# Two transformer blocks on one core: the durations, ranks and one root of a mixer planned while the program is built

## The chip, the core and the metric

The kernel runs on one core of a Trainium2 chip. The core has five engines with queues of their own: TensorE (PE, matrix products; its weight loads are shown as PEld), VectorE (DVE), ScalarE (ACT), GpSimd (POOL) and SyncE (SP, which here only issues transfers). The metric is the device time of one execution in microseconds (us). The median of three runs of the kernel before is 1177.67 us (1176.16 to 1180.08).

## The reference

The input is a sequence of 256 tokens with 1024 channels. It goes through two blocks of two layers each; every layer is a mixer and an MLP, each with a residual.

```python
# first block: even mixer, MLP, odd mixer, MLP, final norm
h = h + even_mixer(rms_norm(h, mix_norm_g[0]), ...)      # DSA: 8 heads; NSA: 8 heads in 2 groups
h = h + diff_mixer(rms_norm(h, mix_norm_g[1]), ...)      # 8 heads of two score maps
h = h + square(relu(rms_norm(h, mlp_norm_g[l]) @ w_up[l])) @ w_down[l]    # 1024 -> 4096 -> 1024
# second block, modulated by a conditioning vector: pooling mixer, MLP, MoBA attention, MLP, final norm
```

- The even mixer has two halves. In DSA an indexer of four small heads scores all keys, the 64 best of each query are kept, and eight heads attend to them. NSA adds three gated branches: attention to keys that a small MLP (`cmp_w1`, a gelu, `cmp_w2`) compresses from windows of 32 tokens, attention to selected blocks, and attention to a sliding window. With 256 tokens all blocks are selected and the window holds the sequence, so the last two are plain causal attention with keys of their own.
- The odd mixer subtracts a second softmax map, times a learned number, from a first: `a = p[:, :, 0] - lam_val * p[:, :, 1]`. Its output is normed for each head by a root mean square over 128 channels before the output product (`rms_norm(o, subln_g) * (1 - lambda_init)`). This is the sub-norm that the change speaks of.
- The second block's attention has 16 causal heads with a relative bias; with 256 tokens and blocks of 256 there are no past blocks to gather.

## The kernel before

Precision. All large products are made of three: each float32 operand is split into a high and a low half (`whi` and `wlo` of a weight, `xh` and `xl` of the activations), and high x high, low x high and high x low are summed in PSUM (`mm3`, line 383). The weights, 2048 columns of 128 partitions at a time, arrive by transfers from SP into a ring of four `raw` tiles; ACT makes `whi`, DVE makes `wlo` by subtraction, into rings of three. In the mixers a split is done in pieces of 512 columns. Attention itself (scores `sc`, transposes `pT` of the softmax, products `o`) is in plain float32.

Stages. After the first projection the program goes: even mixer, MLP 0, odd mixer, MLP 1, pooling, MLP 2, second block's attention, MLP 3. The MLPs (`mlp`, line 842) are written out in a fixed order, with 16 upward products (`pc`) and 16 downward ones (`dn`), and weight splits spread between their matmuls.

The plan. The three attention mixers have no order written by hand. While the program is built, each piece of work is a Python generator that yields before every group of instructions what it waits for. `Plan.run` (line 274) asks all generators for the earliest time at which their next step could start, takes those within a short tie (`TIE`, 0.12 us) of the earliest, and emits the step of the lowest rank among them. The instruction order that results is fixed; on the chip each engine works through its own queue in that order and waits on semaphores. What sets the order therefore is:

- `Clock` (line 47) and `Watched.cost` (line 141): an estimated time for each engine, advanced by an estimated duration for each instruction, plus a lag until another engine sees a result (`SYNC`, 0.08 us; 0.2 us after a matmul). Nothing of it is on the chip.
- the ranks: pairs of heads have their number in the order of attention, counted from 0 (`g_attend`, line 1061), and the front of that line its number plus 1.5; the projections and output products (`g_main`, `g_d`, `g_chain`; `Gather.gen`) have 80 to 85, so that they fill PE when attention waits; the join of the compressed branch (`g_join`, line 1392) 7; the sub-norm (`g_subln`) 5; the indexer's top-k (`g_top`) 9; the weight splits (`g_high`, `g_low`) -20 while less than 768 columns are ahead of PE, else 90.
- `soonest` (line 347), which picks DVE, ACT or POOL for scaling a softmax and for emptying a transpose, by the estimate plus a handicap for DVE (`DEAR`: 0.3, 0.5 and 0 us in the three mixers).

Details that the prediction's steps touch:

- In the even mixer a column is a pair of NSA heads, one of each group. Its selected and window branches are pairs 2c and 2c + 1. The compressed branch is added straight in PSUM if its softmax `pct` is there by then, else the column is evacuated and listed in `late`, and `g_join` adds the branch afterwards (product `oc`). The column is then split into `opA` and `opB`. The first output product (`dn` from `opA`) needs columns 0 and 1. The transposes of a softmax, the joins and other small products share one PSUM slot (`tp`).
- The compressing MLP (`hps`, in `g_main`, line 1168) multiplies 32 weight slices of 256 columns; four in a row go to four groups of 32 output rows.
- In the odd mixer `g_subln` runs once for each two heads, four times in all. It sums squares on PE (`oss`), computes the inverse root of four columns with `rsqrt_of` (line 649), spreads it over the partitions by transposes (`rw`), scales `osb` on DVE, and splits it on ACT and DVE for the output product. `rsqrt_of` starts from an integer guess (two DVE instructions) and does three Newton rounds on the engine it is given.
- In the second block's attention `g_chain` runs v of the first half, q and k of the second half, v of the second half, one after the other. Each ends with evacuations on ACT (`dv<-pj`, and `dq`, `dk` from `pc`) before the next begins. Pairs 0 to 3 are of the first half of the heads, 4 to 7 of the second.

The root's rounds, as they stand for an engine other than VectorE:

```python
        for _ in range(3):
            tt(t, y, y, ALU.mult, eng)
            tt(t, t, v, ALU.mult, eng)
            if eng is V:
                stt(y, t, 1.5, y, ALU.add, ALU.mult)
            else:
                eng.tensor_scalar(t, t, 1.5, None, op0=ALU.add)
                tt(y, t, y, ALU.mult, eng)
```

Of the kernel before, what the change touches and what calls it, by code (L numbers as in the profile page):

```python
# [38 lines left out]
INF = 1e30  # L39

DEAR = dict(V=0.3), dict(V=0.5), dict()
TOP_RANK, CMP_RANK = 9, -3

SPLIT_AHEAD = 768


class Clock:
# [3 lines left out]
    SYNC, DMA_RATE, DMA_LAG = 0.08, 3.2e5, 2.2  # L51

    def __init__(self):
        self.T = dict(PE=0.0, V=0.0, S=0.0, G=0.0)
        self.dma = 0.0
        self.mem, self.last = {}, {}

# [61 lines left out]

    def load(self, out, n_bytes):  # L120
# [14 lines left out]
class Watched:  # L135
# [5 lines left out]
    def cost(self, fn, out, ins, k, aps):  # L141
        size = Clock.size
        n = size(out)
        if self.name == "V":
# [4 lines left out]
            if fn == "tensor_tensor_reduce":  # L149
                return 0.25 + 1.0e-3 * n  # L150
# [4 lines left out]
            if fn == "reciprocal":  # L155
                return 0.15 + 0.7e-3 * n
            return 0.15 + 1.03e-3 * n
        if self.name == "S":
            return 0.2 + 0.79e-3 * n + 0.1 * (len(aps) > 2) + 0.19 * ("accum_out" in k)
        if fn == "tensor_scalar":  # L160
            return 0.2 + 3.4e-3 * n
        return 0.2 + 2.2e-3 * n

    def __getattr__(self, fn):
        real, clock = getattr(self.eng, fn), self.clock

        def call(*a, **k):
# [10 lines left out]
            if fn == "matmul":  # L178
                out, w, x = aps[:3]
                n = Clock.size(x)  # L180
                if x.dtype == F32:
                    dur, lag = max(0.11, n / 600.0 + 0.004), 0.2
                else:
                    dur, lag = 0.0092 + 0.4324e-3 * n, 0.2
                clock.note("PE", dur, [out], [w, x], lag)
            elif fn == "transpose":
                clock.note("PE", 0.109, aps[:1], aps[1:], 0.2)
# [60 lines left out]
class Plan:  # L248
# [3 lines left out]
    TIE = 0.12  # L252

    def __init__(self, clock):
        self.clock, self.q, self.n = clock, [], 0
# [18 lines left out]
    def run(self, until):  # L274
        while not until():
# [3 lines left out]
            self.advance(min((e for t, e in es if t <= m + self.TIE), key=lambda e: (e[0]() if callable(e[0]) else e[0], e[1])))  # L279
# [3 lines left out]
def two_blocks_kernel(ctx: ExitStack, tc: tile.TileContext, A, out):  # L283
# [25 lines left out]
    class Planned:  # L309

        on, dear = False, {}

        def __init__(self, dear):
            Planned.dear = dear

        def __enter__(self):
# [4 lines left out]
            for f in (g_high, g_low):  # L321
                plan.add(f(), lambda: -20 if W.ahead() < SPLIT_AHEAD else 90)
# [24 lines left out]
    def soonest(costs, *aps):  # L347

        return min(costs, key=lambda e: clock.at(e, *aps) + costs[e] + Planned.dear.get(e, 0.0))
# [679 lines left out]
    class Pair:  # L1029
# [5 lines left out]
        def scores(self):  # L1035

            t = clock.T["PE"]
# [15 lines left out]
    def attend(pairs):  # L1053
        at = [0]

        def front():
            return at[0] + 1.5
# [16 lines left out]
    def pv_pair(ps, pTs, vs, first, last):  # L1074

        t = clock.T["PE"]
# [4 lines left out]
        clock.T["PE"] = max(t, clock.T["PE"] - 0.55)  # L1081
# [86 lines left out]
    def g_main():  # L1168

        hps = None  # L1170
        for key in ORDER0[1:]:
            c = key[1]
            if key[0] == "w1":
# [4 lines left out]
                for it in range(2):  # L1178
# [923 lines left out]
```

## Time and profile before

| what | value |
|---|---|
| median of three runs | 1177.67 us |
| the profiled execution's own time | 1175.99 us |
| its span, first to last instruction | 1174.2 us |
| mean granted PE clock | 0.987 |
| PE busy | 1133.7 us, 97% |
| DVE, ACT, POOL busy | 855.7, 642.6, 41.4 us |
| moved by transfers | 243.91 MB, 208 GB/s in the mean |

An instruction row names engine, operation, output tile <- input tiles (buffer numbers left out), and shapes. Almost all instructions are issued by helpers, so their line is the same (L168); one goes by tiles. A busy PE is not a PE at full speed: matmuls overlap in the pipeline, so the distance from start to start is what one costs, and the granted clock (1.0 is full speed) says how fast the array ran. A float32 matmul of attention shows as several rows. In brackets behind a row stands the engine's idle time before it and the instruction that ended it.

### The profile page before, as it was taken

What the parts mean: (1) busy time and instruction counts of PE and PEld (TensorE: products, weight loads), DVE (VectorE), ACT (ScalarE), POOL (GpSimd) and SP (SyncE); (2) the same over time, 40 slices, a digit from 0 to 9 for tenths busy, and PEclk for the clock granted to TensorE, in tenths of its full rate; (3) what the DMA queues carried; (4) which work ended last, traced back from release to release, by engine and by line L of the source; (5) the groups of instructions that cost most, each with busy time, mean ns of one, the idle gap of its engine ahead of it and who ended that gap; (6) DMA issues with size and microseconds to landing.
All of it is one profiled execution on the core that took longest, in us unless ns stands there. A gap on an engine that the chain in (4) does not pass through costs nothing.

```text
span 1174.2 us, 21778 instructions
## 1 busy us (share of the span) xinstructions
PE 1133.7 (97%) x8760; PEld 1066.8 (91%) x8760; DVE 855.7 (73%) x1769; ACT 642.6 (55%) x1169; POOL 41.4 (4%) x113
## 2 busy tenths in 40 slices
PE   8997999999999998999999999999998999999997
PEld 6764899999987788999999999999996889999997
DVE  6967788777778776877787887777698558645554
ACT  6566664544455664545444664545466556555543
POOL 1200000000010203000000100000000000000000
PEclk9998999999999998999999999999999999999998
DMA  9520468888855434688888258888642444555530
GB/s 347 208 109 1 144 216 298 302 285 300 308 186 214 144 108 163 210 312 291 303 297 291 74 206 295 304 299 296 216 144 97 155 148 145 195 195 180 180 108 36
DMA packets 43476, 243.91 MB, mean 208 GB/s; under 512 B 5536, under 2 KB 6192, under 8 KB 21104
## 3 DMA queue, kind: packets, MB, share of 16 engines
q1 hardware_dynamic: 42336, 239.58, 58.3%
q0 software_dynamic: 896, 2.91, 0.8%
q8 instruction: 68, 1.11, 0.4%
q14 instruction: 32, 0.26, 0.1%
q10 hardware_dynamic: 144, 0.05, 0.0%
HBM read 241.44 MB, written 1.07 MB: 207 GB/s over the span
## 4 chain that ended last, share of the span: by engine, by line
PE 86%; DVE 7%; POOL 2%; ACT 2%; issue 1%; DMA 1%; SPq 0%; DVEq 0%; ACTq 0%; POOLq 0%
PE dn L168 37%; PE pc L168 32%; PE pj L168 9%; PE sc L168 2%; DVE wlo L168 2%; PE o L168 2%; PE pT L168 2%; POOL rs_t L168 1%; DMA raw<-in_in_c_dram 1%; DVE rs_t L168 1%; PE tps L168 1%; ACT whi L168 1%; DVE sq L168 0%; DVE x L168 0%; SPq L168 0%
## 5 line engine op out<-in xcount | busy, mean ns | idle before, releaser
L168 DVE TENSOR_TENSOR wlo<-raw,whi 128x1024 fp32r<-128x1024 f32 (+2 forms) x440 | 421.8, 997 | 123.6 <-ACT whi L168 123.1
L168 ACT ACTIVATE whi<-raw 128x1024 fp32r<-128x1024 f32 (+2 forms) x440 | 360.0, 869 | 128.2 <-PE dn L168 100.3
L168 PE MATMUL pc<-xh,whi 128*128 128x256 f32 (+1 forms) x1152 | 327.1, 284 | 1.4 <-DVE bias L168 1.4
L168 PE MATMUL pc<-xl,whi 128*128 128x256 f32 (+1 forms) x1152 | 325.8, 283 | 0.0
L168 PE MATMUL pc<-xh,wlo 128*128 128x256 f32 (+1 forms) x1152 | 325.1, 282 | 0.0
L168 PE MATMUL dn<-hh,whi 128*128 128x256 f32 x1024 | 289.7, 283 | 1.7 <-DVE bias L168 1.7
L168 PE MATMUL dn<-hl,whi 128*128 128x256 f32 x1024 | 289.4, 283 | 1.7 <-DVE hl L168 1.7
L168 PE MATMUL dn<-hh,wlo 128*128 128x256 f32 x1024 | 289.5, 283 | 0.0
L168 PEld LDWEIGHTS pc<-xh,whi 128*128 128x128 f32 x1152 | 217.7, 189 | 2.5 <-issue 2.3
L168 PEld LDWEIGHTS pc<-xh,wlo 128*128 128x128 f32 x1152 | 217.8, 189 | 0.0
L168 PEld LDWEIGHTS pc<-xl,whi 128*128 128x128 f32 x1152 | 217.8, 189 | 0.0
L168 PEld LDWEIGHTS dn<-hl,whi 128*128 128x128 f32 x1024 | 195.9, 191 | 2.1 <-DVE hl L168 2.1
L168 PEld LDWEIGHTS dn<-hh,whi 128*128 128x128 f32 x1024 | 195.9, 191 | 2.0 <-issue 2.0
L168 PEld LDWEIGHTS dn<-hh,wlo 128*128 128x128 f32 x1024 | 195.9, 191 | 0.0
L168 DVE SCALAR_TENSOR_TENSOR graw<-graw,cact 128x1024 f32<-128x1024 f32 x96 | 116.1, 1219 | 20.8 <-DMA graw<-in_w_mod_dram 20.7
L168 ACT ACTIVATE hh<-r 128x512 fp32r<-128x512 f32 x64 | 40.5, 633 | 127.1 <-DVE r L168 126.1
L168 PE MATMUL pj<-whi,xh 128*128 128x512 f32 (+2 forms) x208 | 86.1, 414 | 5.0 <-ACT whi L168 5.0
L168 ACT ACTIVATE r<-sc,bias 128x256 f32<-128x256 f32 x64 | 29.1, 502 | 112.5 <-DVE bias L168 112.5
L168 PE MATMUL pj<-wlo,xh 128*128 128x512 f32 (+2 forms) x208 | 80.8, 388 | 0.2 <-DVE wlo L168 0.2
L168 PE MATMUL pj<-whi,xl 128*128 128x512 f32 (+2 forms) x208 | 80.6, 387 | 0.0
L168 DVE TENSOR_TENSOR sc<-pc,rb 128x256 f32<-128x256 f32 x72 | 29.4, 417 | 36.6 <-PE pc L168 36.5
L168 PEld LDWEIGHTS pj<-whi,xh 128*128 128x128 f32 x208 | 39.6, 191 | 14.8 <-ACT whi L168 6.0
(262 smaller groups left out, 1290.6 us busy)
## 6 DMA issues: line engine op xcount, KB each, us to landing
raw<-in_up_dram SPq DMA_DIRECT2D x64, 1024.0 KB, 5.6
raw<-in_down_dram SPq DMA_DIRECT2D x64, 1024.0 KB, 5.4
graw<-in_w_mod_dram SPq DMA_DIRECT2D x96, 512.0 KB, 5.3
raw<-in_in_d_dram SPq DMA_DIRECT2D x12, 1024.0 KB, 5.5
raw<-in_w_out_dram SPq DMA_DIRECT2D x8, 1024.0 KB, 5.0
raw<-in_qk_dram SPq DMA_DIRECT2D x8, 1024.0 KB, 5.0
raw<-in_in_c_dram SPq DMA_DIRECT2D x7, 1024.0 KB, 8.9
raw<-in_v_dram SPq DMA_DIRECT2D x4, 1024.0 KB, 4.8
```

The source lines that it names most:

```text
L168: r = real(*a, **k)
```

## The change

- Durations: `Watched.cost` gets other constants for several instructions (among them the reciprocal, which now grows by 6.3 ns for each column, and fixed parts of POOL's); a float32 matmul counts at least 0.2 us; the lag after a matmul is 0.16, `SYNC` 0.05 us. A new function `turn` adds 0.09 us when PE goes from a split product to a float32 one or back. Where matmuls run side by side, the corrections are set anew.
- The parameters of the three mixers (`STRETCH`): handicap of DVE, columns ahead below which splits come first, distance of the front of the attention line, and the tie. Before they were 0.3, 0.5, 0 / 768 / 1.5 / 0.12 throughout.
- Ranks: top-k 9 to 12; `g_join` 7 to 3; the heads of the odd mixer's q and k from 20 to 8 (30 to 18 for the second half); `g_subln` 5 to 0; the projections of the second block's attention 85 to 3.
- The root in `g_subln` runs on VectorE.
- The compressing MLP's four row groups are emitted in one step, and three of four count 0.01 us each.

```diff
-DEAR = dict(V=0.3), dict(V=0.5), dict()
-TOP_RANK, CMP_RANK = 9, -3
-SPLIT_AHEAD = 768
+TOP_RANK, CMP_RANK = 12, -3
+STRETCH = (0.6, 384, 1.5, 0.3), (0.0, 1280, 1.5, 0.2), (0.3, 512, 2.5, 0.06)
...
-    SYNC, DMA_RATE, DMA_LAG = 0.08, 3.2e5, 2.2
+    SYNC, DMA_RATE, DMA_LAG = 0.05, 3.2e5, 2.2
...
+    def turn(self, kind):
+        if kind != self.kind:
+            self.T["PE"] += 0.09
+        self.kind = kind
...
             if fn == "reciprocal":
-                return 0.15 + 0.7e-3 * n
-            return 0.15 + 1.03e-3 * n
+                return 0.14 + 6.3e-3 * n
+            return 0.15 + 1.03e-3 * n if n < 64 or n > 256 else 0.24 + 0.92e-3 * n
...
         if fn == "tensor_scalar":
-            return 0.2 + 3.4e-3 * n
-        return 0.2 + 2.2e-3 * n
+            return 0.25 + 3.4e-3 * n
+        return 0.2 if n == 2 else 0.35 + 2.0e-3 * n
...
                 if x.dtype == F32:
-                    dur, lag = max(0.11, n / 600.0 + 0.004), 0.2
+                    dur = max(0.2, n / 600.0 + 0.004)
...
+                clock.turn(x.dtype == F32)
+                clock.note("PE", dur, [out], [w, x], 0.16)
...
         def scores(self):
...
-            clock.T["PE"] = t = max(t, clock.T["PE"] - 0.55)
...
-            clock.T["PE"] = max(t, clock.T["PE"] - 0.25)
+            clock.T["PE"] -= 0.5
...
         def front():
-            return at[0] + 1.5
+            return at[0] + Planned.front
...
-                        yield on("PE", w1(kk), L["X"][c])
+                        if k % 4 == 0:
+                            yield on("PE", *[w1(q) for q in range(kk, kk + 4)], L["X"][c])
+                        t = clock.T["PE"]
                         mm(hps[j:j + 32, c * 256:(c + 1) * 256], L["X"][c][:, 32 * k:32 * k + 32],
                            w1(kk), c == 0 and k < 4, k >= 12)
+                        if k % 4:
+                            clock.T["PE"] = t + 0.01
...
-            plan.add(g_join(c), 7)
+            plan.add(g_join(c), 3)
...
-        plan.add(g_flag(g_heads(ps, L["tabs"], 2 - 2 * j, halves_of(dst), (acc_p, tp_p)), ("qk"[j], half)), 20 + 10 * half)
+        plan.add(g_flag(g_heads(ps, L["tabs"], 2 - 2 * j, halves_of(dst), (acc_p, tp_p)), ("qk"[j], half)), 8 + 10 * half)
...
-            r = rsqrt_of(v, 4, G)
+            r = rsqrt_of(v, 4)
...
-                    plan.add(g_subln(hp), 5)
+                    plan.add(g_subln(hp), 0)
...
-        plan.add(g_chain(g_v(0), g_qk(1), g_v(1)), 85)
+        plan.add(g_chain(g_v(0), g_qk(1), g_v(1)), 3)
```

More of the change, by code (lines that the diff above doesn't have):

```diff
@@ L56, in __init__ @@
         self.mem, self.last = {}, {}
+        self.kind = False
     @staticmethod
@@ L149, in cost @@
             if fn == "tensor_tensor_reduce":
-                return 0.25 + 1.0e-3 * n
+                return 0.23 + 1.05e-3 * n
             if fn in ("max", "tensor_reduce"):
@@ L155, in cost @@
             if fn == "reciprocal":
-                return 0.15 + 0.7e-3 * n
-            return 0.15 + 1.03e-3 * n
+                return 0.14 + 6.3e-3 * n
+            return 0.15 + 1.03e-3 * n if n < 64 or n > 256 else 0.24 + 0.92e-3 * n
         if self.name == "S":
-            return 0.2 + 0.79e-3 * n + 0.1 * (len(aps) > 2) + 0.19 * ("accum_out" in k)
+            return 0.2 + 0.79e-3 * n + (0.1 if len(aps) > 2 and "accum_out" not in k else 0.13 * ("accum_out" in k))
+        if fn == "memset":
+            return 0.1 + 0.83e-3 * n
         if fn == "tensor_scalar":
-            return 0.2 + 3.4e-3 * n
-        return 0.2 + 2.2e-3 * n
+            return 0.25 + 3.4e-3 * n
+        return 0.2 if n == 2 else 0.35 + 2.0e-3 * n
     def __getattr__(self, fn):
@@ L181, in call @@
                 if x.dtype == F32:
-                    dur, lag = max(0.11, n / 600.0 + 0.004), 0.2
+                    dur = max(0.2, n / 600.0 + 0.004)
                 else:
-                    dur, lag = 0.0092 + 0.4324e-3 * n, 0.2
-                clock.note("PE", dur, [out], [w, x], lag)
+                    dur = 0.0092 + 0.4324e-3 * n
+                clock.turn(x.dtype == F32)
+                clock.note("PE", dur, [out], [w, x], 0.16)
             elif fn == "transpose":
-                clock.note("PE", 0.109, aps[:1], aps[1:], 0.2)
+                clock.turn(True)
+                clock.note("PE", 0.109, aps[:1], aps[1:], 0.16)
             else:
@@ L248 @@
 class Plan:
-    TIE = 0.12
     def __init__(self, clock):
-        self.clock, self.q, self.n = clock, [], 0
+        self.clock, self.q, self.n, self.tie = clock, [], 0, 0.0
     def add(self, gen, rank):
@@ L309, in two_blocks_kernel, with __init__ @@
     class Planned:
-        on, dear = False, {}
-        def __init__(self, dear):
-            Planned.dear = dear
+        on, dear, ahead, front = False, 0.0, 0, 0.0
+        def __init__(self, dear, ahead, front, tie):
+            Planned.dear, Planned.ahead, Planned.front = dear, ahead, front
+            plan.tie = tie
         def __enter__(self):
@@ L321, in __enter__ @@
             for f in (g_high, g_low):
-                plan.add(f(), lambda: -20 if W.ahead() < SPLIT_AHEAD else 90)
+                plan.add(f(), lambda: -20 if W.ahead() < Planned.ahead else 90)
         def __exit__(self, *a):
@@ L347, in soonest @@
     def soonest(costs, *aps):
-        return min(costs, key=lambda e: clock.at(e, *aps) + costs[e] + Planned.dear.get(e, 0.0))
+        return min(costs, key=lambda e: clock.at(e, *aps) + costs[e] + (Planned.dear if e == "V" else 0.0))
     def act(o, i, func=AF.Copy, **k):
@@ L1035, in scores @@
         def scores(self):
-            t = clock.T["PE"]
             for u in self.us:
@@ L1080, in pv_pair @@
             mm(ps[64 * i:64 * i + 64, 128:256], vs[i][1], pTs[i][:, 256:384], False, last)
-        clock.T["PE"] = max(t, clock.T["PE"] - 0.55)
+        clock.T["PE"] -= 0.46
     def g_split(ps, oh, ol):
@@ L1422, in g_top @@
                 mm(pss[g][:, 256:384], qs[g][:, 0:128], ki[half_rows[g], 0:128], False, True)
-            clock.T["PE"] -= 0.7
+            clock.T["PE"] -= 0.5
             for g in range(2):
@@ L1497, in fin @@
                         if L.get("pct"):
-                            plan.add(g_join(c), 7)
+                            plan.add(g_join(c), 3)
                         else:
@@ L1524, in two_blocks_kernel @@
     W.size = PIECE_ATT
-    with Planned(DEAR[0]):
+    with Planned(*STRETCH[0]):
         w2ks.hold(st.sq[0], *proj0)
@@ L1716, in two_blocks_kernel @@
     t0 = clock.T["PE"]
-    with Planned(DEAR[1]):
+    with Planned(*STRETCH[1]):
         w2ks.hold(lamt_, *oht_)
```

7 lines of the change are left out of this document (3 added, 4 removed).

## The prediction

> **What bounds the kernel now.** I read the page first: span, share of each engine, granted clock by slice, and the chain that ended last.
>
> ```profile
> span 1174.2 us, 21778 instructions
> PE 1133.7 (97%) x8760; PEld 1066.8 (91%) x8760; DVE 855.7 (73%) x1769; ACT 642.6 (55%) x1169; POOL 41.4 (4%) x113
> PEclk9998999999999998999999999999999999999998
> PE 86%; DVE 7%; POOL 2%; ACT 2%; issue 1%; DMA 1%; SPq 0%; DVEq 0%; ACTq 0%; POOLq 0%
> ```
>
> PE is the bound, so an order that only shifts other engines is worth nothing; what counts is time in which PE idles or runs at a reduced clock. Of the 14% of the chain off PE, POOL has 2%, though it is busy for 4% of the span. PEclk dips in slices that lie in the even mixer (about 90 to 120 us) and at the end of the odd one (about 446 to 458 us). The change touches three stretches alone: the even mixer (A, about 22 to 149 us), the odd one (B, 335 to 464 us) and the attention of the second block (C, 880 to 976 us). The MLPs between are not planned and stay as they are.
>
> Next, windows over the two dips and the hole in C; columns are length, then busy time of PE, weight load, DVE, ACT, POOL, then granted clock, DMA share, GB/s.
>
> ```profile
> 90.00:95.00 5.00, 2.33 (x18) 1.45 (x16) 4.10 (x16) 2.79 (x10) 0.35 (x2) 0.97 0.00 0
> 95.00:100.00 5.00, 3.65 (x16) 2.05 (x16) 4.71 (x16) 1.71 (x4) 0.00 (x0) 0.50 0.00 0
> 100.00:105.00 5.00, 5.00 (x23) 3.40 (x23) 1.23 (x6) 2.68 (x9) 0.20 (x1) 0.50 0.00 0
> 105.00:110.00 5.00, 3.34 (x24) 2.22 (x24) 3.87 (x20) 3.77 (x12) 0.20 (x1) 1.00 0.01 2
> 110.00:116.00 6.00, 3.68 (x31) 2.15 (x32) 5.90 (x28) 4.29 (x16) 0.39 (x2) 1.00 0.01 1
> ...
> 446.00:450.00 4.00, 2.94 (x14) 2.79 (x14) 3.93 (x9) 2.15 (x5) 3.17 (x7) 0.54 0.24 37
> 450.00:454.00 4.00, 3.19 (x16) 2.90 (x16) 1.00 (x3) 0.00 (x0) 3.17 (x11) 0.50 0.66 254
> 454.00:458.00 4.00, 4.00 (x25) 4.00 (x25) 1.21 (x2) 0.63 (x1) 0.53 (x2) 0.68 0.96 299
> ...
> 896.00:902.00 6.00, 2.66 (x20) 1.94 (x20) 5.37 (x27) 4.96 (x18) 0.00 (x0) 1.00 0.00 1
> ```
>
> A, 90 to 116: PE is busy for 18.0 of 26 us, so 8.0 idle, and 8.65 of that busy time is at clock 0.50, half of which, 4.3, is lost: 12.3 us in all. B, 446 to 458: the lost share of the clock is 2.94 x 0.46 + 3.19 x 0.50 + 4.00 x 0.32 = 4.2 us. C, 896 to 902: 3.3 idle.
>
> **B: the sub-norm's root.** Four times (once for each two heads) the root ran as 13 POOL instructions: one on v, then three rounds of four. All 52 go. VectorE gets 10 each: one and three rounds of three, since it fuses add and multiply. The trace has this chain on both engines: the first rows are a sub-norm, the others the same function, two columns wide, on VectorE.
>
> ```profile
> 445.97 0.16 DVE L168 TENSOR_SCALAR rs_v<-oss 128x4 f32<-128x4 f32 x1 [0.54 <-PE oss L168]
> 446.62 0.59 POOL L168 TENSOR_TENSOR rs_t<-rs_y 128x4 f32<-128x4 f32 x1
> 451.76 0.20 POOL L168 TENSOR_TENSOR rs_y<-rs_t,rs_y 128x4 f32<-128x4 f32 x1
> 452.01 1.12 PE L168 MATMUL rw<-kc,rs_y 128*128 128x128 f32 x4 [0.81 <-POOL rs_y L168]
> ...
> 866.16 0.15 DVE L168 TENSOR_SCALAR rs_v<-ss 128x2 f32<-128x2 f32 x1
> 868.12 0.16 DVE L168 TENSOR_TENSOR rs_t<-rs_t,rs_v 128x2 f32<-128x2 f32 x1
> 868.79 0.38 PE L168 MATMUL rw<-kc,rs_y 128*128 128x128 f32 x2
> ...
> L168 DVE TENSOR_TENSOR rs_t<-rs_y 128x2 f32<-128x2 f32 (+1 forms) x27 | 4.4, 161 | 0.6
> ...
> PE rw L168 <- POOL rs_y L168: 2.1, 2, 1.6
> ...
> PE rw L168 <- POOL rs_y L168: 2.5, 2, 1.6
> PE dn L168 <- DVE xl L168: 1.1, 1, 1.1
> ```
>
> From the first instruction to the transposes: 452.01 - 445.97 = 6.04 us on POOL, 868.79 - 866.16 = 2.63 on VectorE, 3.4 sooner. The longest PE wait for a root is 1.6, so each of the four could vanish: 2.1 + 2.5 = 4.6. What is late next is the chain behind it, the scaling of osb, its split on ACT and VectorE, and the output product's 96 matmuls; the 1.1 for xl is that chain. Since the third chain moves earlier by as much as the fourth, I take 4.0 of the 4.6 and 0.5 of the 1.1. The gate opened again only at about 456 us; with the holes at 443 and 447 filled most of the 4.2 should return: I take 3.0. **B: 4.0 + 0.5 + 3.0 = 7.5 us**; at most 4.6 + 1.1 + 4.2 = 9.9. VectorE pays 4 x 10 x 0.161 = 6.4 us, under the projections' and output products' matmuls; queued behind each block stand softmax steps, the weights' low halves and xl, on which the next matmuls wait. If that cover is gone, up to 6.4 come onto the path: 9.9 - 6.4 = 3.5, or 4.6 + 1.1 - 6.4 = -0.7 if the clock stays low as well; these are the bad ends. POOL's queue after the last root holds the four loads for the pooling; they start earlier, into a stretch with a DMA share of 0.24 to 0.66.
>
> What brings the clock back is not certain. [...] No single wait quoted above is longer than 1.6, yet the clock was 0.54; the trace thus has the gate closing on scattered holes. [...]
>
> **A: a join at rank 3, and better durations.** The compressed branch of column 0 is joined late. PE in 105 to 117 us:
>
> ```profile
> 106.85 0.55 PE L168 MATMUL pT<-kc,p 128*128 128x128 f32 x3 [0.58 <-ACT pTs L168]
> 108.09 0.55 PE L168 MATMUL pT<-kc,p 128*128 128x128 f32 x3 [0.70 <-ACT pTs L168]
> ...
> 110.42 0.55 PE L168 MATMUL pT<-kc,p 128*128 128x128 f32 x3 [0.58 <-ACT pTs L168]
> 111.61 0.65 PE L168 MATMUL oc<-dv,dq 120*64 120x256 f32 x4 [0.65 <-DVE pTs L168]
> 113.51 0.55 PE L168 MATMUL pT<-kc,p 128*128 128x128 f32 x3 [1.25 <-ACT p L168]
> ...
> 116.18 0.36 PE L168 MATMUL dn<-opA,whi 128*128 128x256 f32 x1
> ...
> 103.23 0.38 ACT L168 ACTIVATE opA<-o 128x256 fp32r<-128x256 f32 x1 [1.61 <-PE o L168]
> 113.36 0.40 ACT L168 ACTIVATE opA<-z 128x256 fp32r<-128x256 f32 x1
> ```
>
> Column 1 is split at 103.23, column 0 only at 113.36, after its join (oc) at 111.61: that sat at rank 7, behind transposes of pairs of lower rank that share its one PSUM slot. So the first output product waited to 116.18, while PE idled 5.00 - 3.34 + 6.00 - 3.68 = 4.0 us after 105. At rank 3 the join goes ahead of the pairs numbered 4 to 7, and 48 matmuls are there from about 104 to fill these holes. Each fill turns PE to the other kind of matmul and back; from two rows below, 89.73 - 89.41 = 0.32 against the usual 0.23 between such matmuls, a turn costs 0.09: six holes, 1.1 us. So 4.0 - 1.1 = 2.9.
>
> ```profile
> 89.17 0.40 PE L168 MATMUL pj<-wlo,xh 128*128 128x512 f32 x1
> 89.41 0.39 PE L168 MATMUL pj<-whi,xl 128*128 128x512 f32 x1
> 89.73 0.92 PE L168 MATMUL sc<-z,dq 64*128 64x256 f32 x8
> ```
>
> The other 8.3 of the 12.3 (4.0 idle and 4.3 of clock before 105) needs projections kept back as filler, which no edit does directly (g_main stays at rank 85): 0.5. The compressing MLP's four row-group matmuls now come out in one step and cost the estimate one matmul, not four; they run side by side, so a group no longer broken saves some tenths: 0.6 in all. **A: 2.9 + 0.5 + 0.6 = 4.0 us.** Bounds: 12.3 + 0.6 = 12.9 at the good end; at the bad end the filler is missing later, and the 4.0 idle moves behind 116 and 4.0 is lost. Wider ties (0.3) and the later split (ahead 384) only choose among these.
>
> **C: the projections' chain from rank 85 to 3.**
>
> ```profile
> 896.32 0.58 ACT L168 ACTIVATE dv<-pj 128x512 f32<-128x512 f32 x1
> 899.79 0.52 PE L168 MATMUL pT<-kc,p 128*128 128x128 f32 x3 [1.05 <-ACT p L168]
> 900.98 0.58 ACT L168 ACTIVATE dv<-pj 128x512 f32<-128x512 f32 x1
> 902.96 0.39 PE L168 MATMUL pc<-xh,whi 128*128 128x256 f32 x1
> ```
>
> The two evacuations of v (896.32, 900.98) had rank 85 on ACT, behind every softmax, and the next projection (pc) waits for both in its chain: hence the 3.3 of idle. At rank 3 they pass the pairs from 3 on, not the first three. **C: 2.0 us** of the 3.3. The bad end: projections run ahead and the last pairs stand alone, below.
>
> **Sum.** 7.5 + 4.0 + 2.0 = 13.5. The profiled execution took 1175.99 (1.8 around its span of 1174.2): 1162.5. The median of the runs is 1177.67, 1.7 more: **1164.2 us**.
>
> **Rivals.**
> 1. B alone pays; A and C reshuffle evenly: 1177.67 - 7.5 = 1170.2. For it: better durations are not by themselves a better order, since the plan takes one step at a time and never looks ahead.
> 2. Everything comes back: 9.9 + 12.3 + 3.3 = 25.5, 1152.2. Against it: the filler for 90 to 104 is not provided by name.
> 3. The clock does not hang on the short holes: B 4.5, A 3.5 (its reshuffling 0.5 gone), C 2.0: 1167.7. [...]
> 4. The wait moves: behind the root stand the scaling and splits, and VectorE's 6.4 us delays them; B 3.5, and six turns of 0.09 more in A and C: 1177.67 - 3.5 + 0.5 = 1174.7, no measurable change.
> 5. Slower: the filler is spent early in C. With projections at rank 3, the second half's pairs come after them with only output products to cover; C then gets a stretch like A's 90 to 116, 12.3 us, and A gives nothing: 1177.67 + 12.3 - 7.5 = 1182.5. It decides from a loss of 7.5 + 3.5 us on. Against it: two output products of the first half, 96 matmuls, are free by then.
>
> **How the numbers follow.** The forecast's own mechanism 0.34, rivals 1 to 5: 0.22, 0.10, 0.12, 0.12, 0.10. Faster, that is, below 1174.1 (0.3%, about what a measurement of this kernel can tell): 0.34 + 0.22 + 0.10 + 0.12 = 0.78; same 0.12; slower, above 1181.2, 0.10. The range leaves out half of rival 2 and most of rival 5: 1154 to 1178.
>
> **What would show it.** B: rw no longer waits for POOL rs_y, oss to rw is 2.6 us, clock 1.0 between 440 and 460. A: oc before 104 us, first dn before 107, less idle in its place. C: no idle of over 1 us between v and the first pc. Wrong would be: a half-clock stretch of 10 us at the end of B or C, DVE as releaser of rw or of dn in B, or A ending no earlier than 149 us after the start.

## The result

The kernel after takes 1148.94 us in the median of four runs (1147.5 to 1149.74); the kernel before, with one more run beside it, 1176.91 (four runs, 1174.3 to 1180.08). The ratio is 0.976, its 95% interval 0.9732 to 0.9787: faster by 28 us, about twice the 13.5 that the sum gave, and below the range's lower end of 1154.

First the page of the kernel after: span, PE's busy time, the granted clock by slice, and the shares of the chain that ended last.

```profile
span 1145.6 us, 21749 instructions
...
PE 1121.4 (98%) x8760; PEld 1061.0 (93%) x8760; DVE 855.0 (75%) x1790; ACT 648.7 (57%) x1186; POOL 25.0 (2%) x61
...
PEclk9999999999999999999999999999999999999999
...
PE 88%; DVE 6%; ACT 3%; issue 1%; DMA 1%; POOL 1%; SPq 0%; DVEq 0%; ACTq 0%; POOLq 0%
```

PE executes the same 8760 rows in 12.3 us less, and no slice of PEclk dips any more.

To see where the 28.6 us of the span (1174.2 to 1145.6) went, I cut both traces at marks that do not depend on the plan. Stage A ends with the first upward product (`pc`) of MLP 0 and is counted from the start of the span (its window leaves out the first 12 us). B goes from the last `pc` of MLP 0 to the first of MLP 1, C from the first q and k product of the second block's attention to the first `pc` of MLP 3. Before, then after; the columns are those of the prediction's windows (length, busy time of each engine with its count, granted clock, DMA share, GB/s).

```profile
12.00:151.79 139.79, 129.04 (x865) 98.93 (x864) 110.44 (x368) 90.63 (x254) 11.81 (x36) 0.95 0.42 157
318.92:463.85 144.93, 138.94 (x833) 119.47 (x832) 108.60 (x288) 83.68 (x202) 22.59 (x62) 0.96 0.48 167
854.64:975.20 120.56, 114.96 (x857) 101.97 (x855) 85.52 (x258) 73.96 (x185) 0.00 (x0) 1.00 0.41 141
```

```profile
12.00:138.09 126.09, 121.80 (x866) 96.00 (x864) 103.97 (x350) 94.64 (x267) 12.03 (x36) 1.00 0.46 170
305.72:440.90 135.18, 134.81 (x833) 115.52 (x832) 116.28 (x335) 81.52 (x195) 6.04 (x10) 1.00 0.51 181
831.64:946.47 114.83, 113.41 (x857) 102.82 (x855) 82.48 (x248) 77.55 (x195) 0.00 (x0) 1.00 0.44 149
```

| stage | length before, after | gain | of it PE's idle time (length less busy) | of it PE's busy time | predicted |
|---|---|---|---|---|---|
| A | 151.8, 138.1 | 13.7 | 10.75 to 4.29: 6.5 | 129.04 to 121.80: 7.2 | 4.0 |
| B | 144.9, 135.2 | 9.8 | 5.99 to 0.37: 5.6 | 138.94 to 134.81: 4.1 | 7.5 |
| C | 120.6, 114.8 | 5.7 | 5.60 to 1.42: 4.2 | 114.96 to 113.41: 1.6 | 2.0 |

The three gains make 29.2, the whole of the 28.6 and 0.6 more. The stretch between A and B, an MLP, is as long as before: 318.92 - 151.79 = 167.1 and 305.72 - 138.09 = 167.6. PE's busy time shrinks with no matmul less, in A and B mostly because the clock rose from 0.95 and 0.96 to 1.00: by the rows of the last section 11.99 and 8.51 us of the busy time before were at half clock. Half of that, 6.0 and 4.3 us, I take as lost (the output product's matmuls start 0.21 us apart at half clock, from 447.59 to 450.79, and 0.12 apart at full clock, from 456.55 to 456.91), against the 7.2 and 4.1 that came back. Where C's 1.6 us come from, at a clock of 1.00 before and after, is not shown.

The windows that answer to the prediction's, in the kernel after: the middle of A, the tail of B, and C at about the same distance from its start (872 - 831.64 = 40.4; before 896 - 854.64 = 41.4).

```profile
90.00:95.00 5.00, 4.68 (x34) 2.93 (x33) 3.88 (x21) 5.00 (x21) 0.53 (x3) 1.00 0.01 2
95.00:100.00 5.00, 4.23 (x31) 2.54 (x29) 3.92 (x23) 4.38 (x14) 0.46 (x3) 1.00 0.00 0
100.00:105.00 5.00, 4.59 (x35) 3.86 (x36) 4.83 (x22) 4.39 (x15) 0.40 (x2) 1.00 0.02 3
...
424.00:428.00 4.00, 4.00 (x34) 3.95 (x34) 3.50 (x13) 0.66 (x2) 1.07 (x2) 1.00 0.81 270
872.00:878.00 6.00, 6.00 (x53) 6.00 (x52) 4.53 (x13) 4.71 (x16) 0.00 (x0) 1.00 0.54 176
```

Between 90 and 105 PE was busy for 10.98 of 15 us, mostly at half clock; now for 13.5 at full clock. The row from the tail of B and the one from C have no idle time at all. All waits of PE on another engine that the trace lists in B and in C (in total, times, longest) are these two; the second lies within the first q and k products, and the kernel before has it there too, as long:

```profile
PE o L177 <- DVE nm L177: 0.3, 1, 0.3
...
PE pc L177 <- DVE bias L177: 1.4, 1, 1.4
```

Marks that the prediction named for A and B, in the timeline of the kernel after (start, duration, engine, operation):

```profile
102.15 0.39 PE L177 MATMUL dn<-opA,whi 128*128 128x256 f32 x1
...
426.77 0.16 DVE L177 TENSOR_SCALAR rs_v<-oss 128x4 f32<-128x4 f32 x1 [0.33 <-PE oss L177]
...
429.26 0.62 PE L177 MATMUL rw<-kc,rs_y 128*128 128x128 f32 x4
```

The last root takes 429.26 - 426.77 = 2.49 us (2.6 predicted) and PE does not wait for it. The first output product of A stands at 102.15 (before 107 predicted). But the join `oc`, which was to bring that, does not occur in this trace at all: the compressed branch comes early enough to be added in PSUM for every column. The forecast's end was seen, and not its way.

### The profile page after: what moved, and what is told of

The parts are those of the page before. It is cut to its first block, busy times and chain, and to the rows that moved or that the text cites. A ratio compares the mean times of both kernels' runs of the same rounds, so it can differ in the third digit from the quotient of the medians.

```text
span 1145.6 us, 21749 instructions
## 1 busy us (share of the span) xinstructions
PE 1121.4 (98%) x8760; PEld 1061.0 (93%) x8760; DVE 855.0 (75%) x1790; ACT 648.7 (57%) x1186; POOL 25.0 (2%) x61
## 4 chain that ended last, share of the span: by engine, by line
PE 88%; DVE 6%; ACT 3%; issue 1%; DMA 1%; POOL 1%; SPq 0%; DVEq 0%; ACTq 0%; POOLq 0%
PE dn L177 37%; PE pc L177 33%; PE pj L177 10%; DVE wlo L177 2%; PE o L177 2%; PE sc L177 2%; PE pT L177 1%; DMA raw<-in_in_c_dram 1%; ACT p L177 1%; ACT whi L177 1%; DVE rs_t L177 1%; DVE x L177 1%; DVE sq L177 1%; PE tps L177 0%; SPq L177 0%
## 5 line engine op out<-in xcount | busy, mean ns | idle before, releaser
L177 ACT ACTIVATE p<-p,nm 128x128 f32<-128x128 f32 x112 | 49.5, 446 | 6.3 <-DVE nm L177 6.3
```

The source lines that it names most:

```text
L177: r = real(*a, **k)
```

## The experiments

Every kernel below computes the whole function. They differ in the order of instructions, in the engine that `soonest` picks for a scaling or an evacuation, and, where it is said, in the engine of the root. Stage lengths come from one profiled execution each; executions of one kernel differ by some us (the four of e1 took 1166.36 to 1170.81 us, and its stages are those of the first). The times are to be read beside runs of the kernel before on the same chip: 1175.68 us (median of 7) for e1 to e4, 1176.03 for e5 to e8, 1176.06 for e9, 1178.41 for e10 to e12, and 1177.35 (median of 6) for e13 and e14.

| kernel | time, us | A | B | C |
|---|---|---|---|---|
| before | 1176.91 | 151.8 | 144.9 | 120.6 |
| after | 1148.94 | 138.1 | 135.2 | 114.8 |
| e1: one edit in each stage | 1169.2 | 146.9 | 143.4 | 117.2 |
| e2: after, without these | 1157.52 | 142.3 | 136.4 | 119.2 |
| e3: durations alone | 1157.81 | 140.7 | 138.2 | 117.0 |
| e4: after, durations undone | 1169.11 | 143.3 | 150.0 | 114.8 |
| e5: durations of PE alone | 1178.24 | 148.0 | 149.3 | 117.9 |
| e6: all others alone | 1175.03 | 149.2 | 144.6 | 119.1 |
| e7: ranks alone | 1182.74 | 148.6 | 151.1 | 122.8 |
| e8: after, parameters undone | 1152.65 | 141.1 | 136.3 | 114.9 |
| e9: before, tie 0.10 / 0.15 | 1170.35 / 1173.07 | 149.7 / 147.5 | 141.5 / 148.3 | 120.2 / 118.6 |
| e9: durations alone, tie 0.10 / 0.15 | 1158.54 / 1164.58 | 141.9 / 144.5 | 139.7 / 137.7 | 116.6 / 121.3 |
| e10: PE's and POOL's durations | 1167.44 | 144.2 | 145.0 | 117.9 |
| e11: all durations but POOL's | 1162.87 | 141.2 | 142.8 | 117.0 |
| e12: the compressing MLP's one wait alone | 1171.37 | 146.4 | 142.9 | 122.1 |
| e13: after, ranks undone | 1149.15 | 137.8 | 135.6 | 114.8 |
| e14: after, other ties | 1153.43 | 140.3 | 138.1 | 115.5 |

One kernel proves little here: any edit reshuffles the order far beyond its own place, and the tie alone moves A by up to 4.3 us, B by 6.8 and C by 4.7 (e9 below). Sets of kernels say more. With all the new durations (eight kernels: after, e2, e3, e8, two of e9, e13, e14) B is 135.2 to 139.7, in the other eleven 141.5 to 151.1. In C the six kernels with the projections at rank 3 have 114.8 to 117.2, the other thirteen 116.6 to 122.8. In A both the durations and the compressing MLP's step count: 137.8 to 141.1 with both (after, e8, e13, e14), 140.7 to 144.5 with the durations without the step (e2, e3, two of e9), 146.9 and 143.3 with the step on the old durations (e1, e4), 147.5 to 151.8 with neither (before, e7, two of e9).

**One edit in each stage, alone (e1) and undone (e2).** The stages are apart in time, so one kernel tests three edits: the compressing MLP's step in A, the root in B, the chain's rank in C.

```diff
 e1, against before
+                        if k % 4 == 0:
+                            yield on("PE", *[w1(q) for q in range(kk, kk + 4)], L["X"][c])
+                        ...
+                            clock.T["PE"] = t + 0.01
-            r = rsqrt_of(v, 4, G)
+            r = rsqrt_of(v, 4)
-        plan.add(g_chain(g_v(0), g_qk(1), g_v(1)), 85)
+        plan.add(g_chain(g_v(0), g_qk(1), g_v(1)), 3)
 e2, against after: the same lines the other way round
```

> The kernel before with one edit in each planned stretch: even mixer (A) the compressing MLP's four row groups in one step, three of them counted 0.01 us; odd mixer (B) the root on VectorE; second block's attention (C) the projections at rank 3. Lengths in the traces, before and after the change: A, up to the first pc of MLP 0, 151.8 and 138.1 us; B, last pc of MLP 0 to first pc of MLP 1, 145.0 and 135.2; C, first to last pc gap of the attention (854.6 to 975.2), 120.6 and 114.9. Theory of the new traces (the compressed branch came 17 us sooner, so the join of the prediction does not occur at all): A falls to 143 or less by this edit alone, hps takes under 4.5 us from first to last. Rival, the prediction's own step (A gains by the join's rank): A stays at 148 or more. B: theory of the prediction, the root alone gives at least 7 of the 9.8, B at 138 or less; rival, ranks and durations give it, B at 141 or more. C: theory, rank 3 alone removes the idle between v and the first pc, C at 117 or less; rival, it needs the new front and durations, C stays above 119 or gets longer.

> The changed kernel without those three edits. If each is what pays: A goes back to 146 or more, B to 142 or more with a stretch at half clock at its end, C to 118 or more. If the durations, ties and other ranks pay: A stays within 2 us of 138.1, B of 135.2, C of 114.9.

e1 took 1169.2 us, ratio 0.9943 [0.9927, 0.9959]; e2 1157.52, ratio 0.9845 [0.9829, 0.9862]. In e1 A lies between the two bounds, B is where the rival put it, and C misses its 117 by 0.2; in e2 A lies between the bounds, B stays within 2 us, as the durations' side said, and C goes back over 118, as the edit's side said. By stage, each edit alone and what its removal from the kernel after costs: the compressing MLP's step 4.9 and 4.2 us (A), the root 1.5 and 1.2 (B), the chain's rank 3.4 and 4.4 (C). So the root, the largest item of the prediction, shows the least, too little to tell from a shuffle; among the eight kernels with the new durations B is 135.2 to 138.1 with the root on VectorE and 136.4 to 139.7 with it on POOL. The longest waits of PE in B of e1 (in total, times, longest) show why, after the wait for the root in B of before:

```profile
PE rw L168 <- POOL rs_y L168: 4.5, 4, 1.6
...
PE rw L168 <- DVE rs_y L168: 1.7, 1, 1.7
PE dn L168 <- ACT xh L168: 1.5, 1, 1.5
PE pT L168 <- DVE osb L168: 0.8, 1, 0.8
```

POOL is gone as a releaser, and VectorE, xh and osb have taken its place: 4.0 us in these three and 5.3 in all, against 5.9 in all before. And a half clock remains in B of e1, 6.83 us (436.46 to 443.29) instead of 10.24. In B of e2, where the root is still on POOL, but the durations are new:

```profile
PE rw L177 <- POOL rs_y L177: 0.9, 2, 0.6
```

Of the 4.5 us of waiting 0.9 are left though no root was moved; the only other wait there has 0.3.

The compressing MLP's step was the surprise in A. Rows of the matmuls hps (last slices), pcT and, between 50 and 70 us, one of the three kinds of projection matmuls; count, durations, first and last start. Before:

```profile
L168 PE MATMUL hps<-raw,dk x16: 379/379/403, 63.1 to 69.2; 128*32 128x256 f32 x16
L168 PE MATMUL pcT<-kc,pc x2: 421/430/439, 95.8 to 96.0; 128*120 128x128 f32 x2
L168 PE MATMUL pj<-whi,xl x3: 387/392/395, 49.9 to 51.3; 128*128 128x512 f32 x3
```

After:

```profile
L177 PE MATMUL hps<-raw,dk x16: 379/379/379, 56.8 to 57.5; 128*32 128x256 f32 x16
L177 PE MATMUL pcT<-kc,pc x2: 272/298/325, 78.8 to 79.0; 128*120 128x128 f32 x2
L177 PE MATMUL pj<-whi,xl x17: 390/395/405, 49.7 to 69.9; 128*128 128x512 f32 x17
```

The MLP ends 11.7 us sooner (69.2 to 57.5), the softmax of the compressed branch 17 us sooner (95.8 to 78.8), and the projections behind the MLP in the same generator start before 70 instead of after. That is what the step moves, not its own matmuls (e1, with the step alone, has the softmax at 78.9 as well). In e1 it could have paid more: PE stood still for a whole 3.42 us there and then ran 10.24 us at half clock, as its windows show.

```profile
112.20:115.60 3.40, 2.06 (x19) 1.69 (x17) 3.40 (x19) 0.00 (x0) 0.00 (x0) 1.00 0.01 2
115.60:119.02 3.42, 0.00 (x0) 0.00 (x0) 3.24 (x15) 0.00 (x0) 0.00 (x0) 1.00 0.00 0
119.02:129.26 10.24, 9.51 (x37) 6.85 (x39) 6.50 (x35) 7.01 (x28) 0.00 (x0) 0.50 0.01 2
```

**The durations alone (e3) and undone (e4).**

```diff
 e3, against before: Clock, turn, Watched.cost and the corrections of after; e4, against after: those of before
-    SYNC, DMA_RATE, DMA_LAG = 0.08, 3.2e5, 2.2
+    SYNC, DMA_RATE, DMA_LAG = 0.05, 3.2e5, 2.2
...
-                return 0.15 + 0.7e-3 * n
+                return 0.14 + 6.3e-3 * n
...
```

> The kernel before with nothing but the new durations, lags and the 0.09 us turn in the estimate (ranks, parameters, root, row groups as before). Theory (one edit in each stretch does it): all three stretches within 3 us of before, A 149 to 155, B 142 to 148, C 118 to 124. Rival (a truer estimate gives the better order): at least two of them take more than half of the gain, A under 145, B under 140, C under 118.

> The changed kernel with the durations, lags and turn of before. Theory: little is lost, A under 142, B under 138, C under 117. Rival (the durations carry the gain): the stretches come back by more than half, A over 145, B over 140, C over 118.

e3 took 1157.81 us, 17.9 less than before; e4 1169.11, 20.2 more than after. In e3 all three stages are within the rival's bounds. In e4 only B is: it loses 14.8 us, A 5.2, between the two bounds, and C nothing, as the theory said. There the root is on VectorE and the durations are old, and PE's longest waits in B are:

```profile
PE rw L168 <- DVE rs_y L168: 2.5, 1, 2.5
PE rw L168 <- DVE r L168: 1.7, 1, 1.7
```

No instruction is added or taken away in e3; only their order differs, and for some scalings and evacuations the engine that `soonest` picks. The three stages of e3:

```profile
12.00:140.67 128.67, 123.63 (x864) 95.32 (x862) 107.95 (x360) 93.88 (x265) 11.76 (x36) 1.00 0.45 170
307.79:446.00 138.21, 135.33 (x834) 115.62 (x833) 108.99 (x287) 84.47 (x203) 21.30 (x62) 1.00 0.52 178
840.03:956.99 116.96, 114.23 (x856) 101.94 (x855) 84.92 (x256) 74.64 (x187) 0.00 (x0) 1.00 0.42 146
```

The clock is 1.00 in A and B as in the kernel after, and PE's idle time in A is 128.67 - 123.63 = 5.0 instead of 10.75. This A owes nothing to an earlier compressed branch: its transpose pcT starts at 98.1 us there (95.8 before), and three columns are joined by oc. How far the old numbers were off, rows of the trace of before tell (busy time and mean ns, or the one duration):

```profile
L168 DVE RECIPROCAL gate<-gate x1: 452/452/452, 36.0 to 36.0; 128x48 f32<-128x48 f32 x1
...
L168 POOL TENSOR_TENSOR rs_t<-rs_y 128x4 f32<-128x4 f32 x12 | 4.5, 377 | 0.6
L168 POOL TENSOR_TENSOR t<-pj,tabs 128x64 f32<-128x64 f32 x4 | 2.1, 546 | 0.0
```

| instruction | old estimate, ns | new | trace |
|---|---|---|---|
| reciprocal of 48 columns on DVE | 150 + 0.7 x 48 = 184 | 140 + 6.3 x 48 = 442 | 452 |
| the step rs_t<-rs_y of the root on POOL, 4 columns | 200 + 2.2 x 4 = 209 | 350 + 2 x 4 = 358 | 377 |
| product of 64 columns on POOL | 200 + 2.2 x 64 = 341 | 350 + 2 x 64 = 478 | 546 |

**Which durations (e5, e6, e10, e11).** e5 has only PE's part of the new estimate (0.2 us for a float32 matmul, `turn`, the lags); e6 the other engines' and `SYNC`; e10 PE's and POOL's; e11 all but POOL's.

```diff
 POOL's part, which is in e6 and e10 and not in e5 and e11
-            return 0.2 + 3.4e-3 * n
-        return 0.2 + 2.2e-3 * n
+            return 0.25 + 3.4e-3 * n
+        return 0.2 if n == 2 else 0.35 + 2.0e-3 * n
```

> The kernel before with only PE's part of the new estimate: the 0.09 us turn, at least 0.2 us for a float32 matmul, the lag of 0.16 and the corrections where matmuls run side by side. The durations alone gave A 140.7, B 138.2, C 117.0 (before 151.8, 144.9, 120.6). Theory (PE was reckoned too fast, a score pair at 0.49 us for a measured 0.85 and no turns, so that filler was spent too early and the end of a stretch ran dry): this part alone gives most of it, B at 140 or less without a half-clock stretch at its end, A at 144 or less, C at 118 or less. Rival (POOL's or ACT's durations do it, for example the root's 13 POOL instructions): B stays over 142 and A over 147.

> The kernel before with the rest of the new estimate: durations of DVE, ACT and POOL, and 0.05 us for a semaphore; PE's as before. Theory (PE's part does it): A, B and C within 3 us of 151.8, 144.9 and 120.6, with a half-clock stretch at the end of B. Rival (the other engines' part): B at 140 or less and A at 144 or less.

> The kernel before with the new durations of PE (float32 matmul, turn, lag) and of POOL, but the old ones of DVE and ACT. Theory (PE's and the vector engines' durations must agree with each other): as with PE's alone, A 146 to 152, B 142 to 150, time 1168 to 1180. Rival (POOL's were what PE's half lacked, since the root of the odd mixer is on POOL): B at most 140, time at most 1168.

> The kernel before with all new durations but POOL's. Theory: near the kernel with all of them, A at most 145, B at most 141, time 1155 to 1166. Rival (POOL's are needed): B at least 143, time at least 1166.

Neither half gains (1178.24 and 1175.03, where before took 1176.03). e5 misses its theory in A and B; e6 stays within 3 us of before in all stages, but without the half clock at the end of B. After e5 and e6 I held that all must be true at once; e10 and e11 soften that. e10 at 1167.44 is at the edge of the rival's time, with B as long as the theory said and A shorter; e11 has A as short as with all, and B between the two bounds. So the gain comes in steps. A is 148.0 and 149.2 with the halves, 144.2 with PE's and POOL's, 141.2 with all but POOL's; next to the 4 us by which the tie alone moves A, this doesn't tell which addition counts. POOL's have one clear effect, on the root. PE's wait for it in B without POOL's durations, e5 and e11:

```profile
PE rw L175 <- POOL rs_y L175: 5.0, 3, 2.1
```

```profile
PE rw L175 <- POOL rs_y L175: 5.0, 4, 1.8
```

and with them, e10 and e3:

```profile
PE rw L177 <- POOL rs_y L177: 1.7, 2, 0.9
```

```profile
PE rw L177 <- POOL rs_y L177: 1.8, 3, 0.9
```

In both pairs 3.2 to 3.3 us of the wait go. Over all kernels with the root on POOL the wait is 3.7 to 5.0 us in the seven without POOL's new durations and 0.9 to 3.2 in the six with them, e6 among these (3.2). My reading is that the plan, knowing how long the root is, emits other work for PE meanwhile.

**A truer estimate or a lucky order (e9)?** The plan takes one step at a time, so any edit reshuffles hundreds of instructions. The tie was changed from 0.12 us in the kernel before and in the one with the durations alone.

```diff
-STRETCH = (0.3, 768, 1.5, 0.12), (0.5, 768, 1.5, 0.12), (0.0, 768, 1.5, 0.12)
+STRETCH = (0.3, 768, 1.5, 0.10), (0.5, 768, 1.5, 0.10), (0.0, 768, 1.5, 0.10)
```

> The kernel before with a tie of 0.10 us instead of 0.12 and nothing else; PE's order differs in several hundred places. Theory (the new durations give a better order because they are truer): a slightly different tie with the old durations stays bad, A at least 147 us, B at least 142, time 1170 to 1184. Rival (the order with all new durations was a lucky one among many): the tie alone throws the stages about as far as the durations did, so A or B falls to the level of the durations alone (A 140.7, B 138.2) in some of these kernels, and the ranges of old and new overlap.

> The kernel before with a tie of 0.15 us. Theory: A at least 147 us, B at least 142, time 1170 to 1184. Rival (luck): overlap with the kernels that have the new durations.

> The kernel before with all the new durations and a tie of 0.10 us. Theory: as with a tie of 0.12, A at most 144 us, B at most 140, C at most 119, time 1154 to 1163. Rival (luck): the gain of 18 us falls away with another tie, time 1165 to 1180.

> The kernel before with all the new durations and a tie of 0.15 us. Theory: A at most 144 us, B at most 140, C at most 119, time 1154 to 1163. Rival (luck): 1165 to 1180.

With the old durations A is 147.5 to 151.8 and B 141.5 to 148.3; with the new ones 140.7 to 144.5 and 137.7 to 139.7. The two sets do not overlap in A or B; in C they do (118.6 to 120.6 and 116.6 to 121.3). Some bounds were missed: B 141.5 for "at least 142", and with the new durations and a tie of 0.15 A 144.5 for 144, C 121.3 for 119 and the time 1164.58 for 1163. The means of the three, the kernel before and e3 among them, are 1173.4 ((1176.91 + 1170.35 + 1173.07) / 3) and 1160.3 ((1157.81 + 1158.54 + 1164.58) / 3): about 13 us belong to the truer durations. In the same means A gains 7.3 us, B 6.4 and C 1.5; some 2 of these 15.2 us are lost again outside the three stages, in e3 between B and C (last section). The tie alone moves a kernel by up to 6.8 us (1157.81 to 1164.58), so the 18 us of e3 hold some luck, and so does a stage difference of 4 us between two kernels.

**Ranks and parameters (e7, e8, e13, e14).** e7 is before with the join at 3, the sub-norm at 0, the heads of q and k at 8 and the parameters of C; e8 after with the old parameters; e13 after with the old ranks of join, top-k, sub-norm and heads; e14 after with other ties.

```diff
 e7, against before (e13, against after, has these three and TOP_RANK the other way round)
-            plan.add(g_join(c), 7)
+            plan.add(g_join(c), 3)
...
-halves_of(dst), (acc_p, tp_p)), ("qk"[j], half)), 20 + 10 * half)
+halves_of(dst), (acc_p, tp_p)), ("qk"[j], half)), 8 + 10 * half)
...
-                    plan.add(g_subln(hp), 5)
+                    plan.add(g_subln(hp), 0)
 e14, against after
-STRETCH = (0.6, 384, 1.5, 0.3), (0.0, 1280, 1.5, 0.2), (0.3, 512, 2.5, 0.06)
+STRETCH = (0.6, 384, 1.5, 0.25), (0.0, 1280, 1.5, 0.25), (0.3, 512, 2.5, 0.08)
```

> The kernel before with ranks or parameters alone: in A the join of the compressed branch at rank 3 (the step of the prediction), in B the sub-norm at rank 0 and the heads of q and k at 8 and 18, in C the parameters of the changed kernel (0.3, 512, 2.5, 0.06) without the chain's rank. The prediction's step says A 148.9, with oc before 104 us and the first output product before 107. Rival (the join is late because everything before it is): A over 150.5, oc comes no more than 3 us sooner. B and C: within 2 us of 144.9 and 120.6 if the durations carry the gain.

> The changed kernel with the parameters of before (handicap 0.3, 0.5, 0; 768 columns; front 1.5; tie 0.12) in all three stretches. Theory (durations and the row groups carry the gain): A 140 or less, B 138 or less, C 117 or less. Rival (the parameters are worth as much as the durations): A over 144, B over 139, C over 118.

> The kernel after with the old ranks of the joins (7), the top-k (9), the sub-norm (5) and the heads of the odd mixer's q and k (20); all else new. Theory (these ranks are not what gained): A and C as after within 1 us, since no join occurs there, B 134 to 138, time 1147 to 1152. Rival (the ranks carry the rest of the gain): A at least 140 or B at least 139, time at least 1153.

> The kernel after with ties of 0.25, 0.25 and 0.08 us instead of 0.3, 0.2 and 0.06. If the new durations make a good order in general: time 1149 to 1156, A 138 to 142, B 135 to 139, C 115 to 118. If the order after was a chosen one whose neighbours are no better than the kernel before with the new durations: time at least 1157.

e7 took 1182.74 us, 6.7 more than before: with the old durations A gains 3.2 by the join, B loses 6.2 by the sub-norm and heads, and C 2.2 by its parameters, the last two beyond the 2 us expected. A and the first output product (106.8 us) are as the prediction's step says, and so is the join, whose matmuls there are:

```profile
L168 PE MATMUL oc<-dv,dq x4: 631/632/634, 101.6 to 102.7; 120*64 120x256 f32 x4
```

In the kernel after these ranks change nothing that can be told: e13 took 1149.15 us, ratio 0.9754 [0.9723, 0.9785], with all stages where its theory put them. The parameters are worth 3.7 us (e8, 1152.65; A is 1.1 over its bound, B and C are within theirs), and the ties alone 4.5 (e14, 1153.43, ratio 0.9797 [0.9773, 0.9822], time and stages as expected of durations that make a good order in general); none of these neighbours is measurably faster, so the kernel after is among the better of near orders. Without the three edits of e2 the parameters and the other ranks gain nothing (1157.52 with them, 1157.81 without in e3).

**The compressing MLP's one wait (e12).** The four row groups wait once, but each counts a whole matmul in the estimate.

```diff
-                        yield on("PE", w1(kk), L["X"][c])
+                        if k % 4 == 0:
+                            yield on("PE", *[w1(q) for q in range(kk, kk + 4)], L["X"][c])
```

> The kernel before, whose compressing MLP waits once for four row groups, each of which still counts a whole matmul in the estimate. If the grouped wait is what counts: hps in 5 us or less, A 145 to 148 as with the whole step. If the count of 0.01 is what counts: hps still spread over 10 us or more and A 149 or more.

```profile
L168 PE MATMUL hps<-z,dk x16: 379/392/404, 51.2 to 52.6; 128*32 128x256 f32 x16
...
L168 PE MATMUL hps<-raw,dk x16: 379/379/404, 63.2 to 63.9; 128*32 128x256 f32 x16
```

The first and last rows of hps in e12 are 12.7 us apart, as the count's side expected, but A is 146.4, as the wait's side did. A's gain of 5 us came with the wait alone, though the tie moves A by as much as 4.3; the count of 0.01 shortens hps further, and what it adds to the time stays open, since e1 lost its part to the standstill shown above. B and C, which this edit doesn't touch, came out 2.0 us shorter and 1.5 longer than before: the shuffle again.

## Why the prediction was wrong

The direction was right and the size was not. Point by point:

- **"The other 8.3 of the 12.3 needs projections kept back as filler, which no edit does directly: 0.5."** This is the step that failed. I took the durations for a shuffle of choices. With nothing but the durations (e3) A loses 11.1 us, its clock is 1.00 and half of its idle time is gone; in the mean of three ties it loses 7.3, and the two sets of A lie apart. So the filler did not have to be named by an edit: a plan whose durations of PE and of the other engines are nearer the trace placed its projections so that more of the holes were filled. Neither half of the durations did it alone (148.0 and 149.2).
- **The join at rank 3, 2.9 us.** Right by itself, but not what happened: in e7 it gave 3.2, close to the sum, though within a shuffle, with `oc` moved from 111.6 to 101.6 and the first output product from 116.2 to 106.8. In the kernel after there is no join left to move, because the branch is there 17 us sooner, and with the ranks taken back (e13) the time is the same.
- **The compressing MLP's step, 0.6 us.** Mis-sized: 4.9 alone and 4.2 undone. I priced its matmuls, not what stands behind them in the generator: the projections and the compressed branch. That they run side by side the rows show: in the kernel after 16 of them, 379 ns each, start between 56.8 and 57.5 us.
- **B, 7.5 us: near in size (9.8 came), wrong in its cause.** The root on VectorE is as fast as said (2.49 us), but was worth 1.5 and 1.2 us, since the wait moved to VectorE's queue, xh and osb, my rival 4 for this edit alone, whose 3.5 was still too much. Most of the 4.5 us of waiting and all of the clock's 4 us came back through the durations, with the root on POOL too (e2: B 136.4; e3, with the durations alone: 138.2).
- **C, 2.0 us.** The mechanism was right (3.4 alone, 4.4 undone), the size too small: I took 2.0 of the one hole at 896 to 902, 3.3 us, where the whole stage had 5.6 us of idle time, of which 4.2 went, and 1.6 us of PE's busy time went with it. Rival 5, the filler spent early in C, did not come; C has only one wait of PE of 1.4 us left.
- **The chances.** Rival 2, that everything comes back, got 0.10 and 1152.2 us, and was the nearest to the 1148.94, by stage too (12.3, 9.9 and 3.3 against 13.7, 9.8 and 5.7). What spoke against it was the step in the first point.
- **Rival 3, that the clock does not hang on short holes,** falls: in A and B the clock returned to 1.00 with the holes filled (the last section has how busy PE was in the windows ahead of a half clock). My reading of the clock in B was too simple all the same: the 3.41 us ahead of its half clock hold not only holes, but also 1.05 us of products one column wide, and what these have to do with it no run varied.

What stays open: which single duration of PE, DVE and ACT carries A; a test of one at a time was not made, and with shuffles of 4 us and more a single kernel would not tell it.

## What to carry to other kernels

Where an order is planned by an estimate, measure the estimate against the trace before weighing ranks: a term that is off by a factor of two (a reciprocal, a small instruction on POOL) costs waits that look like an engine's fault, and correcting the number can be worth more than moving the work. Price a stage by PE's whole idle time and lost clock in it, not by its most visible hole, and price a moved step by what stands behind it. With a greedy plan a single reordered kernel says little within a few microseconds; change something irrelevant (the tie) on both sides before believing a difference.

## What the runs showed of the hardware

The half clock, which the prediction calls a closed gate, lasted 3.41 us or two or three times that in the rows below and in e1, and needed no long standstill ahead of it. The three half-clock periods in the stages of the kernel before, each with the 3.41 us ahead of it:

```profile
53.80:57.21 3.41, 1.44 (x17) 0.59 (x6) 3.34 (x9) 0.57 (x2) 0.00 (x0) 0.99 0.00 0
57.21:60.62 3.41, 3.41 (x19) 2.24 (x21) 2.05 (x5) 0.80 (x2) 0.00 (x0) 0.50 0.00 0
...
91.28:94.69 3.41, 1.09 (x6) 0.62 (x6) 3.20 (x12) 1.88 (x5) 0.35 (x2) 1.00 0.00 0
94.69:104.93 10.24, 8.58 (x37) 5.38 (x37) 6.22 (x23) 4.63 (x14) 0.20 (x1) 0.50 0.00 0
...
442.88:446.29 3.41, 2.64 (x19) 2.24 (x19) 1.63 (x4) 1.97 (x5) 0.37 (x2) 1.00 0.82 298
446.29:456.53 10.24, 8.51 (x38) 8.22 (x39) 5.88 (x11) 2.49 (x5) 6.87 (x17) 0.50 0.59 172
```

PE was busy for 1.44, 1.09 and 2.64 of 3.41 us in the window ahead, and the clock was then 0.50 for 3.41, 10.24 and 10.24 us, one, three and three such windows. In e1, quoted above, the half clock followed a window with no matmul at all, and not the one before it, with 2.06 of 3.40 us busy. So 77% busy was followed by the half clock and 60% was not. But 1.05 of those 2.64 us are a run of products one column wide:

```profile
444.88 1.05 PE L168 MATMUL oss<-ones,sqo 128*128 128x1 f32 x8
```

The clock of the kernel before changes at 57.18, 60.59, 94.72, 104.96, 446.29, 456.53 and 1166.51 us: the distances are 1, 10, 3, 100, 3 and 208 times 3.413 us. Cut into windows of this length, counted from these changes, and after's from its one change at 1140.22 us, the two traces have 661 windows at full clock from about 10 us on. In three of them PE was busy for less than half (42% at 53.76 and 32% at 91.31 us in the kernel before, 29% at 1136.81 in the kernel after), and the half clock followed each. In eight PE was busy for 55 to 60% (from 108.37, 405.33, 661.33, 872.96, 893.44 and 900.27, and after's from 638.47 and 850.09), and it followed none. Of the other 650, all above 60%, it followed two: the one of 77% at 442.88 and one of 98% at 1163.09, which also has products one column wide (ss, 1.95 us from 1164.03 on). Such products alone do not bring it: the window from 398.51 to 401.92 holds 0.95 us of oss with PE busy throughout, and the clock stayed at 1.00. What else decides it is not shown; no run varied these products by themselves.

A half clock came without any idle time ahead of it, too. In e3, at the start of the pooling mixer, which no edit touches:

```profile
633.51:636.92 3.41, 3.41 (x32) 3.41 (x32) 1.60 (x4) 2.75 (x6) 0.00 (x0) 1.00 0.02 5
636.92:643.75 6.83, 6.83 (x34) 6.83 (x34) 5.23 (x20) 2.32 (x6) 0.00 (x0) 0.50 0.43 154
...
634.77 4.85 PE L177 MATMUL ss<-fw,sq 128*128 128x2 f32 x32
```

PE is busy throughout, in the window ahead too, but from 634.77 on only with ss, float32 products of two columns, which begin 1.26 us after the start of that window. The same work is followed by the half clock in e13 as well:

```profile
628.52:631.92 3.40, 3.40 (x33) 3.40 (x31) 1.58 (x4) 2.73 (x6) 0.00 (x0) 1.00 0.01 2
631.92:638.75 6.83, 6.83 (x34) 6.83 (x34) 5.32 (x20) 2.30 (x6) 0.00 (x0) 0.50 0.47 154
```

The kernel after has a clock of 1.00 there:

```profile
629.68 3.63 PE L177 MATMUL ss<-fw,sq 128*128 128x2 f32 x32
```

Its ss begins 1.45 us after the start of a window (628.23 to 631.64); that of the kernel before, also at a clock of 1.00, begins at 652.63, 1.54 us after the start of its window at 651.09. Whether the place in the window decides it was not shown. e3 pays for it: from the end of B to the start of C it takes 394.0 us (446.00 to 840.03), the kernel before 390.8 (463.85 to 854.64) and the kernel after 390.7 (440.90 to 831.64). The mean clock also differs between executions of one kernel: the four of the kernel after have 0.998, 0.995, 0.994 and 0.994, and the trace read here is the first, the fastest; where the others ran slower is not shown.
